# Seven-product groups between single blocks in five feed-forward networks, and 512-column weight splits in the mixers

## The chip, the cores and the metric

One core of one Trainium2 chip. The metric is device time of one execution in microseconds (us), lower is better. Engines: TensorE (PE, its weight loads PEld), VectorE (DVE), ScalarE (ACT), GpSimd (POOL); SyncE (SP) issues the loads.

## The reference

Two transformer blocks over 256 tokens of width 1024, in float32, with five feed-forward networks (FFNs) in all. Each FFN has 2816 hidden columns:

```python
    u = rms_norm(h, norm_ffn_g[l])
    g, up = jnp.split(u @ w_gate_up[l], 2, axis=-1)
    h = h + (jax.nn.silu(g) * up) @ w_down[l]
```

In order: a mixer (attention over 8 heads and an mLSTM, gated, with an output projection), an FFN with a norm behind it; then twice an FFN, a mixer (self attention and attention over 256 memory tokens, with an output projection) and an FFN. The four FFNs of the second part have the same form, with half the result added, `x + 0.5 * swiglu(...)`.

## The kernel before

Tokens stand in two tiles t of 128 rows. A product in float32 is made of three fp32r matmuls: every operand is split into a high part (a cast by ACT) and a low part (source minus high, by DVE), and `mm3` adds high x high, high x low and low x high into one PSUM bank of 512 columns. Activations are split once (`uh`, `ul`; `hh`, `hl` for the hidden block), weights while they stream.

Weights arrive in pieces of 128x2048 (1 MB), loaded in order on SP's queue into three `raw` tiles. Each piece is split in two halves of 1024 columns into `wh` and `wl`, six tiles of each (`W_BUFS`). `half(i, m, n)` hands a half to the matmuls, and makes sure that the splits of the next four jobs (`SPLIT_AHEAD`) have been issued. The order of the jobs is a list, filled beforehand by `plain` (a piece as it is) and `group_jobs`. PE's order is that of the program; ACT, DVE and the queues are ordered by the compiler by priority, with `crit()` moving work 300 places forward.

An FFN is cut into NJ = 11 blocks of 256 hidden columns. For a single block j, `gu(t, j)` runs 24 matmuls (gate and up, 512 columns, 8 row tiles of 128, three each) for each t; `element` makes the hidden block; `turn` transposes it (four 128x128 transposes, one set) and splits it; `dn(t, j)` adds its product with the down weights (12 matmuls for each t) into four PSUM banks that are kept for the whole FFN. So a single costs 72 matmuls. A set of transposes is put into PE's order by a hand-written clock (`side`), some us after the block that it belongs to.

A group takes two blocks j, j+1 with seven products instead of eight (2x2 blocks: token tile t by half of the 1024 inner rows; rows by hidden block). Its products P1, P6, P2, P5, P3, P7, P4 have 12 matmuls each and read sums of weights: DVE adds pieces for P6 (`t2`, four additions of 128x1024 in all), POOL's queue adds two more by accumulating transfers. Between the products stand the `dn` of two earlier blocks a, b, 24 matmuls each. A group costs 7 x 12 + 48 = 132 matmuls, and its results are joined by DVE. `group_operands`, after block 0, makes the sums of the activations.

Before the change an FFN runs five singles (0 to 4) and then three groups (5, 6), (7, 8), (9, 10), and then the down products of the last two blocks (48 matmuls, the tail), in which each of the last blocks is transposed and split in two parts, `turn((0,), j, ..)` and `turn((1,), j, ..)`, whose `hh` tiles have one buffer per t (`bufs=n`; two for the joint turn of both t). `fin(t)` adds the FFN's result to h, and `boundary` transposes and splits it for the next stage (eight transposes per t). `during` lets other work start inside the FFN: the parameters of the second part in the first FFN, the memory tokens' preparation (16 transposes and their splits) in the second and fourth.

The mixers split their 62 pieces (30, 16, 16) by the same code.

Of the kernel before, what the change touches and what calls it, by code (L numbers as in the profile page):

```python
# [19 lines left out]
NJ = 11  # L20
P_FFN = 3 * NJ
# [5 lines left out]
SPLIT_AHEAD = 4  # L27
LOAD_AHEAD = 2
CRIT = 300
SPLIT_W = 1024  # L30

GROUPS = 3

# [81 lines left out]
def kernel(  # L117
# [16 lines left out]
    pe, act, dve, pool = nc.tensor, nc.scalar, nc.vector, nc.gpsimd  # L134
    ctx.enter_context(tc.manual_schedule(engines={mybir.EngineType.PE}))
    side = Order()
# [57 lines left out]
    jobs, at_job = [], {}  # L194

    piece_at = {}

    def add_job(key, piece, work):

# [3 lines left out]
    def plain(i):  # L203
        for m in range(2):
            add_job((i, m), i, lambda i=i, m=m: raws[i][:, 1024 * m:1024 * m + 1024])
# [15 lines left out]
    def split(hi, lo, src):  # L221
        c = act.copy(out=hi, in_=src)  # L222
        dve.tensor_tensor(out=lo, in0=src, in1=hi.bitcast(F32), op=ALU.subtract)  # L223
        return c
# [3 lines left out]
    def in_order(inst):  # L228

        if order[0] is not None:  # L230
            tc.add_manual_dep(inst.ins, order[0].ins.name,
                              mybir.DependencyInfo(mybir.DependencyClass.NoSync, mybir.DependencyReason.DATA),
                              reason="order of the operands")
        order[0] = inst

    def split_to(n):

        while stream["split"] < min(n, len(jobs)):
            key, piece, work = jobs[stream["split"]]
            load_to(piece + 1 + LOAD_AHEAD)  # L240
            r = work()
            hi = wp.tile([128, 1024], FR, tag="wh", bufs=W_BUFS, name="wh")
            lo = wp.tile([128, 1024], FR, tag="wl", bufs=W_BUFS, name="wl")
            for s in range(0, 1024, SPLIT_W):
                in_order(split(hi[:, s:s + SPLIT_W], lo[:, s:s + SPLIT_W], r[:, s:s + SPLIT_W]))
            parts[key] = (hi, lo)
            stream["split"] += 1

# [5 lines left out]
    def group_jobs(i, pool_, dn):  # L254


        b11, b12, b22, b21 = i, i + 2, i + 3, i + 4
        kept[b12] = kept[b22] = pool_
        s = lambda m: slice(1024 * m, 1024 * m + 1024)
        total = []  # L260

        def job(name, piece, work):
            for m in range(2):
                add_job(((i, name), m), piece, lambda m=m: work(m))

        def add(out, a, b):
            dve.tensor_tensor(out=out, in0=a, in1=b, op=ALU.add)  # L267

        def t2(m):
            if m == 0:  # L270
                total.append(pool_[0].tile([128, 2048], F32, tag="tn", bufs=1, name="tn"))
            add(raws[b11][:, s(m)], raws[b11][:, s(m)], raws[b12][:, s(m)])
            add(total[0][:, s(m)], raws[b11][:, s(m)], raws[b22][:, s(m)])
            return total[0][:, s(m)]

        def dma_add(out, a):
            pool.dma_start(out=out, in_=a, accum_op=ALU.add)

        def b21_(m):
            if m == 0:  # L280
                dma_add(raws[b12], raws[b22])
            return raws[b21][:, s(m)]

        def b11_(m):
            if m == 0:
                dma_add(total[0], raws[b21])
            return raws[b11][:, s(m)]

        def t3(m):
            return raws[b12][:, s(m)]  # L290

        def t4(m):
            return total[0][:, s(m)]

        job("P1", b11, lambda m: raws[b11][:, s(m)])
        plain(dn[0])
        job("P6", b22, t2)
        job("P2", b21, b21_)
        job("P5", b21, b11_)
        plain(dn[1])  # L300
        job("P3", b21, lambda m: raws[b22][:, s(m)])
        job("P7", b21, t3)
        job("P4", b21, t4)
# [114 lines left out]
    def ffn_plan(p0):  # L418

        plan = {"pool": [None]}  # L420
        i = p0

        def source(key):
            kind, j = key
            if kind == "dn":
                return p0 + (3 * j + 4 if j < NJ - 1 else 32)
            return p0 if j == 0 else p0 + 3 * j - 1
        nc_ = NJ - 2 * GROUPS

        def take(key, n=1):  # L430
            nonlocal i
            plan[key] = i
            for q in range(n):
                piece_at[i + q] = source(key) + q
            i += n

        for j in range(nc_):
            take(("gu", j), 2)
            if 1 <= j < nc_ - 1:
                take(("dn", j - 1))  # L440
        for j in range(nc_):
            for q in range(2):
                plain(plan["gu", j] + q)
            if 1 <= j < nc_ - 1:
                plain(plan["dn", j - 1])
        for g in range(GROUPS):
            j = nc_ + 2 * g
            a, b = (j - 2, j - 1) if g == 0 else (j - 1, j - 2)
            plan["group", g] = i
            plan["dn", a], plan["dn", b] = i + 1, i + 5  # L450
            g0, g1 = source(("gu", j)), source(("gu", j + 1))
            piece_at.update(enumerate((g0, source(("dn", a)), g1, g1 + 1, g0 + 1, source(("dn", b))), i))
            group_jobs(i, plan["pool"], (i + 1, i + 5))
            i += 6
        for j in ((NJ - 2, NJ - 1) if GROUPS else ()):
            take(("dn", j))
            plain(plan["dn", j])
        assert i == p0 + P_FFN
        return plan

    def ffn_body(fp, p0, u, r, res_scale, finish, during=None):
        plan = plans[p0]
        plan["pool"][0] = fp
        accd = [None, None]
        hidT, hid_ready, hids = {}, {}, {}
        n_conv = NJ - 2 * GROUPS

        def element(t, j, acc):

# [8 lines left out]
        def gu(t, j):  # L478
            i = plan["gu", j]
            acc = lin(u[t], (i, i + 1))  # L480
            element(t, j, acc)
            if t == 1:
                side.spawn(turn((0, 1), j, 3.46))
            side.run()

# [63 lines left out]
            for name, t, k in (("P1", 0, 0), ("P2", 0, 4), ("P4", 1, 4)):  # L549
                S[name] = u[t][0][:, k:k + 4], u[t][1][:, k:k + 4]  # L550

        def group(g):

            j = n_conv + 2 * g
            a, b = (j - 2, j - 1) if g == 0 else (j - 1, j - 2)
            last = g == GROUPS - 1
            i = plan["group", g]

            def joined(x, y, op, into=None):
                o = fp.tile([128, 512], F32, tag="jo", bufs=4, name="jo") if into is None else into  # L560
                with crit():
                    dve.tensor_tensor(out=o, in0=x, in1=y, op=op)  # L562
                return o

            def prod(name):
                acc = bank()
                xh, xl = S[name]
                for k in range(4):
                    wh, wl = half((i, name), k // 2, 512)
                    mm3(acc, xh[:, k], xl[:, k], wh[:, k % 2], wl[:, k % 2], k == 0, k == 3)  # L570
                return acc

            c11 = fp.tile([128, 512], F32, tag="jo", bufs=4, name="jo")
            p1_ = prod("P1")
            with crit():
                act.copy(out=c11, in_=p1_)
            dn(1, a)
            dn(0, a)
            U = joined(prod("P6"), c11, ALU.add)
            joined(prod("P2"), c11, ALU.add, c11)  # L580
            element(0, j, c11)
            if last:
                side.spawn(turn((0,), j, 4.2))
            V = joined(prod("P5"), U, ALU.subtract)
            dn(0, b)
            c12 = joined(prod("P3"), V, ALU.add)
            element(0, j + 1, c12)
            if last:
                side.spawn(turn((0,), j + 1, 4.2))
            dn(1, b)  # L590
            p7 = prod("P7")
            joined(V, p7, ALU.subtract, V)
            element(1, j + 1, V)
            joined(p7, U, ALU.add, U)
            side.spawn(turn((1,) if last else (0, 1), j + 1, 4.9))
            joined(prod("P4"), U, ALU.add, U)
            element(1, j, U)
            side.spawn(turn((1,) if last else (0, 1), j, 4.2))

        for j in range(n_conv):  # L600
            more = 1 <= j < n_conv - 1
            gu(0, j)
            gu(1, j)
            if more:
                dn(0, j - 1)
                dn(1, j - 1)
            if j == 0:
                group_operands()
            if during and j == n_conv - 1:
                during()  # L610
        for g in range(GROUPS):
            group(g)
        j = NJ - 2
        dn(0, j)
        dn(1, j + 1, (0,))
        dn(0, j + 1, by_c=True)
        fin(0)
        dn(1, j + 1, (1,))
        dn(1, j, by_c=True)
        fin(1)  # L620


# [840 lines left out]
    u, r = first_mix(p)  # L1463
# [35 lines left out]
    for layer in range(2):  # L1499
# [7 lines left out]
        with tc.tile_pool(name=f"mix2_{layer}", bufs=1, reuse_waits="tile") as mixp:  # L1507
            u, r = second_mix(mixp, layer, p, nxt["u"], nxt["r"])
# [120 lines left out]
```

## Time and profile before

| | us |
|---|---|
| median of three runs | 1420.66 |
| the three runs | 1420.47, 1420.66, 4846.25 |
| profiled execution | 1421.74 |
| its span, first to last instruction | 1420.0 |
| PE busy in the span | 1369.3 |
| DVE busy | 1102.1 |
| ACT busy | 833.9 |
| POOL busy | 82.9 |

Matmuls overlap in the pipeline and their ends are modelled, so a share of busy time on PE does not tell how near it is to its rate; the distance from one matmul's start to the next does. A wait in a list of waits is idle time of an engine before an instruction, put down to what released it last. Span positions are us from the first instruction.

### The profile page before, as it was taken

The page shows a single profiled execution, that of the slowest core. Times are in us where ns is not written, and L with a number is a line of the kernel's source. Part 1 is how long each engine was busy: PE and PEld are TensorE (multiplying, and loading weights), DVE is VectorE, ACT ScalarE, POOL GpSimd, SP SyncE. Part 2 cuts the span into 40 slices and gives each one's busy share as a digit, 9 for nine tenths or more (in the row PEclk, how much of TensorE's full clock was granted, in tenths as well). Part 3 has the DMA queues.
Part 4 walks back from the last instruction along what each step waited for, and adds up shares of the span by engine and source line. Part 5 has one row for each costly group of instructions (what it writes and reads, how often), then busy time and mean ns, then how long its engine had stood idle before and what let it go on. Part 6 is the DMA issues. An engine that isn't in the chain of part 4 may idle for free.

```text
span 1420.0 us, 17210 instructions
## 1 busy us (share of the span) xinstructions
PE 1369.3 (96%) x6418; PEld 1093.1 (77%) x6418; DVE 1102.1 (78%) x1505; ACT 833.9 (59%) x1208; POOL 82.9 (6%) x89
## 2 busy tenths in 40 slices
PE   8999999999999999999999999999999989999998
PEld 7777888887778877777788877788777757788776
DVE  8866577689985899967585899866998777766897
ACT  6555545466664566567664566554666568554664
POOL 0000000000000000021000000000000111000000
PEclk9999999999999999999999999999999999999999
DMA  8433575477666667553365768656686432566683
GB/s 295 149 132 135 178 252 195 161 237 237 207 222 207 204 193 241 208 200 124 107 237 185 239 178 270 239 207 178 212 248 213 174 107 75 222 208 178 207 252 115
DMA packets 41395, 277.99 MB, mean 196 GB/s; under 512 B 5216, under 2 KB 6240, under 8 KB 8544
## 3 DMA queue, kind: packets, MB, share of 16 engines
q1 hardware_dynamic: 35568, 243.09, 47.2%
q0 software_dynamic: 4320, 31.46, 11.0%
q10 hardware_dynamic: 1424, 2.34, 0.5%
q8 instruction: 50, 0.82, 0.2%
q14 instruction: 33, 0.27, 0.1%
HBM read 244.37 MB, written 1.05 MB: 173 GB/s over the span
## 4 chain that ended last, share of the span: by engine, by line
PE 73%; DVE 18%; ACT 4%; issue 3%; POOL 1%; DMA 1%; DVEq 0%; POOLq 0%; ACTq 0%
PE bank L152 70%; DVE wl L223 8%; PE trbank L157 4%; ACT wh L222 2%; DVE tn L267 2%; POOL fac L341 1%; DVE jo L562 1%; DVE raw L267 1%; DVE hl L223 1%; DVE nm L645 1%; DMA mem<-in_mem_dram 1%; DVE hid L475 1%; DVE ms L1147 0%; ACT hh L222 0%; ACT p L647 0%
## 5 line engine op out<-in xcount | busy, mean ns | idle before, releaser
L223 DVE TENSOR_TENSOR wl<-raw,wh 128x1024 fp32r<-128x1024 f32 x424 | 512.9, 1221 | 132.1 <-ACT wh L222 123.3
L222 ACT CAST wh<-raw 128x1024 fp32r<-128x1024 f32 x424 | 439.0, 1050 | 176.9 <-PE bank L152 159.8
L152 PE MATMUL bank<-wh,uh 128*128 128x512 f32 x948 | 380.7, 402 | 2.2 <-ACT uh L222 2.0
L152 PE MATMUL bank<-wh,ul 128*128 128x512 f32 x948 | 374.5, 395 | 0.2 <-DVE ul L223 0.2
L152 PE MATMUL bank<-wl,uh 128*128 128x512 f32 x948 | 373.2, 394 | 0.0
L152 PEld LDWEIGHTS bank<-wh,uh 128*128 128x128 f32 x948 | 179.6, 189 | 41.9 <-ACT uh L222 2.4
L152 PEld LDWEIGHTS bank<-wh,ul 128*128 128x128 f32 x948 | 179.3, 189 | 40.9 <-DVE ul L223 1.1
L152 PEld LDWEIGHTS bank<-wl,uh 128*128 128x128 f32 x948 | 179.8, 190 | 36.9
L152 PE MATMUL bank<-wh,hh 128*128 128x512 f32 x440 | 176.6, 401 | 6.0 <-ACT hh L222 5.6
L152 PE MATMUL bank<-wh,hl 128*128 128x512 f32 x440 | 173.9, 395 | 4.0 <-DVE hl L223 3.9
L152 PE MATMUL bank<-wl,hh 128*128 128x512 f32 x440 | 173.3, 394 | 3.3 <-DVE wl L223 3.3
L222 ACT CAST wh<-tn 128x1024 fp32r<-128x1024 f32 x60 | 63.1, 1052 | 81.2 <-DVE tn L267 42.5
L152 PEld LDWEIGHTS bank<-wh,hl 128*128 128x128 f32 x440 | 82.6, 188 | 27.9 <-DVE hl L223 10.9
L152 PEld LDWEIGHTS bank<-wh,hh 128*128 128x128 f32 x440 | 82.7, 188 | 26.1 <-ACT hh L222 10.5
L152 PE MATMUL bank<-wl,sh 128*128 128x512 f32 x240 | 95.3, 397 | 6.8 <-DVE wl L223 6.8
L152 PEld LDWEIGHTS bank<-wl,hh 128*128 128x128 f32 x440 | 82.7, 188 | 23.7 <-DVE wl L223 7.6
L152 PE MATMUL bank<-wh,sh 128*128 128x512 f32 x240 | 95.2, 397 | 0.0
L152 PE MATMUL bank<-wh,sl 128*128 128x512 f32 x240 | 94.1, 392 | 0.0
L223 DVE TENSOR_TENSOR wl<-tn,wh 128x1024 fp32r<-128x1024 f32 x60 | 72.9, 1222 | 18.2 <-ACT wh L222 17.4
L223 DVE TENSOR_TENSOR wl<-rawx,wh 128x1024 fp32r<-128x1024 f32 x60 | 70.6, 1218 | 0.8 <-ACT wh L222 0.8
L473 ACT ACTIVATE th<-bank,r 128x256 f32<-128x256 f32 x50 | 23.7, 474 | 77.0 <-PE bank L152 77.0
L562 DVE TENSOR_TENSOR jo<-bank,jo 128x512 f32<-128x512 f32 x90 | 61.7, 686 | 2.1 <-PE bank L152 2.0
(248 smaller groups left out, 1534.0 us busy)
## 6 DMA issues: line engine op xcount, KB each, us to landing
raw<-in_weights_dram SPq DMA_DIRECT2D x196, 1024.0 KB, 4.9
rawx<-in_weights_dram SPq DMA_DIRECT2D x30, 1024.0 KB, 8.2
rawx<-rawx POOLq DMA_DIRECT2D x15, 1024.0 KB, 7.0
tn<-raw POOLq DMA_DIRECT2D x15, 1024.0 KB, 7.7
mem<-in_mem_dram ACTq DMA_DIRECT2D x4, 512.0 KB, 4.4
Tb<-in_rel_dram SPq DMA_DIRECT2D x3, 512.0 KB, 5.9
h<-in_x_dram SPq DMA_DIRECT2D x4, 256.0 KB, 3.8
raw<-in_weights_dram SPq DMA_DIRECT2D x2, 512.0 KB, 5.9
```

Of the source, the lines that this page charges most:

```text
L152: pe.matmul(out=out, lhsT=lhsT, rhs=rhs, start=start, stop=stop)
L157: pe.transpose(out=out, in_=in_, identity=ident if identity is None else identity)
L222: c = act.copy(out=hi, in_=src)
L223: dve.tensor_tensor(out=lo, in0=src, in1=hi.bitcast(F32), op=ALU.subtract)
L267: dve.tensor_tensor(out=out, in0=a, in1=b, op=ALU.add)
L341: pool.tensor_tensor(out=dst, in0=src, in1=mhalf[:, 0:n], op=ALU.pow)
L473: act.activation(out=th, in_=acc[:, 0:256], func=AF.Silu, scale=r[t])
L475: dve.scalar_tensor_tensor(out=hd, in0=acc[:, 256:512], scalar=r[t], in1=th, op0=ALU.mult, op1=ALU.mult)
L562: dve.tensor_tensor(out=o, in0=x, in1=y, op=op)
L645: dve.tensor_reduce(out=nm, in_=s, axis=AX.X, op=ALU.max, negate=True)
```

## The change

`BLOCKS` replaces `GROUPS`: an FFN runs singles 0 and 1, the group (2, 3), single 4, the group (5, 6), single 7, the group (8, 9), and single 10. The down products are taken from a list `todo`: a group carries those of two earlier blocks, a single that of one, and the FFN ends with those of blocks 9, 8 and 10. The last single is transposed in two parts, one for each t; all other blocks for both t together. `during` runs after the fifth of the eight entries, the group (5, 6), instead of after single 4. Pieces of FFNs are noted in `of_ffn` and still split 1024 columns at a time; all others, those of the mixers, 512 at a time.

```diff
-SPLIT_W = 1024
-GROUPS = 3
+SPLIT_W, SPLIT_W_FFN = 512, 1024
+BLOCKS = ((0,), (1,), (2, 3), (4,), (5, 6), (7,), (8, 9), (10,))
...
-            for s in range(0, 1024, SPLIT_W):
-                in_order(split(hi[:, s:s + SPLIT_W], lo[:, s:s + SPLIT_W], r[:, s:s + SPLIT_W]))
+            w = SPLIT_W_FFN if piece in of_ffn else SPLIT_W
+            for s in range(0, 1024, w):
+                in_order(split(hi[:, s:s + w], lo[:, s:s + w], r[:, s:s + w]))
...
+        of_ffn.update(range(p0, p0 + P_FFN))
...
+        todo = []
+        for block in BLOCKS:
+            j = block[0]
+            down = plan["down", j] = [] if len(todo) < 2 else [todo.pop(0) for _ in block]
+            if len(block) == 1:
+                take(("gu", j), 2)
+                for x in down:
+                    take(("dn", x))
+                todo.append(j)
+            else:
+                a, b = down
+                plan["group", j], plan["dn", a], plan["dn", b] = i, i + 1, i + 5
...
+                group_jobs(i, plan["pool"], (i + 1, i + 5))
+                i += 6
+                todo += [j + 1, j]
+        plan["down", None] = todo
+        for x in todo:
+            take(("dn", x))
...
-            if t == 1:
+            if j == BLOCKS[-1][0]:
+                side.spawn(turn((t,), j, 3.46))
+            elif t == 1:
                 side.spawn(turn((0, 1), j, 3.46))
...
-            if last:
-                side.spawn(turn((0,), j, 4.2))
...
-            side.spawn(turn((1,) if last else (0, 1), j + 1, 4.9))
+            side.spawn(turn((0, 1), j + 1, 4.9))
...
-            side.spawn(turn((1,) if last else (0, 1), j, 4.2))
+            side.spawn(turn((0, 1), j, 4.2))
...
+        def single(j):
             gu(0, j)
             gu(1, j)
-            if more:
-                dn(0, j - 1)
-                dn(1, j - 1)
-            if j == 0:
+            for x in plan["down", j]:
+                dn(0, x)
+                dn(1, x)
+
+        for n, block in enumerate(BLOCKS[:-1]):
+            if len(block) == 1:
+                single(block[0])
+            else:
+                group(block[0])
+            if n == 0:
                 group_operands()
-            if during and j == n_conv - 1:
+            if during and n == len(BLOCKS) // 2:
                 during()
-        for g in range(GROUPS):
-            group(g)
-        j = NJ - 2
-        dn(0, j)
-        dn(1, j + 1, (0,))
-        dn(0, j + 1, by_c=True)
+        j = BLOCKS[-1][0]
+        x, = plan["down", j]
+        y, z = plan["down", None]
+        gu(0, j)
+        dn(0, x)
+        gu(1, j)
+        dn(1, x)
+        dn(0, y)
+        dn(1, y, (0,))
+        dn(0, z, by_c=True)
         fin(0)
-        dn(1, j + 1, (1,))
-        dn(1, j, by_c=True)
+        dn(1, y, (1,))
+        dn(1, z, by_c=True)
         fin(1)
```

## Rows read from the trace of the kernel before

**Rows 1.** Timeline of PE: start us, us, engine, line, operation, tiles
```profile
773.72 0.39 PE L152 MATMUL bank<-wl,uh 128*128 128x512 f32 x1
...
776.00 0.39 PE L152 MATMUL bank<-wh,ul 128*128 128x512 f32 x1
```

**Rows 2.** Busy time by stage of the third FFN, columns as headed
```profile
core 0: us, PE busy (x) PEld busy (x) DVE busy (x) ACT busy (x) POOL busy (x), PEclk, DMA share, GB/s
721.85:745.16 23.31, 23.31 (x110) 19.25 (x109) 20.62 (x28) 15.72 (x22) 1.47 (x1) 1.00 0.72 271
745.16:762.08 16.92, 16.92 (x78) 13.91 (x76) 8.84 (x10) 7.64 (x9) 0.00 (x0) 1.00 0.53 187
...
795.93:826.40 30.47, 30.47 (x137) 25.09 (x136) 25.58 (x28) 20.48 (x23) 0.86 (x1) 1.00 0.77 254
826.40:859.34 32.94, 31.94 (x142) 25.48 (x142) 31.79 (x36) 21.17 (x25) 1.72 (x2) 1.00 0.75 233
859.34:893.80 34.46, 32.85 (x146) 25.65 (x144) 32.80 (x37) 22.49 (x27) 1.72 (x2) 1.00 0.72 214
893.80:908.76 14.96, 13.06 (x61) 10.00 (x60) 11.69 (x17) 6.69 (x11) 0.56 (x1) 1.00 0.59 197
```

**Rows 3.** Waits of PE's weight loads, 826.40 to 908.76: us, times, longest
```profile
PEld bank L152 <- DVE wl L223: 3.4, 4, 1.1
PEld bank L152 <- DVE hl L223: 2.5, 4, 1.0
PEld bank L152 <- ACT hh L222: 2.2, 3, 1.3
```

**Rows 4.** Busy time of the five FFNs from the end of gu(1,1)
```profile
236.84:404.14 167.30, 161.25 (x710) 127.88 (x708) 135.15 (x150) 95.36 (x116) 5.98 (x7) 1.00 0.66 213
429.48:597.06 167.58, 162.03 (x725) 129.36 (x724) 137.85 (x155) 96.47 (x119) 6.35 (x8) 1.00 0.67 212
745.16:908.76 163.60, 159.09 (x709) 127.97 (x708) 132.79 (x146) 93.75 (x113) 5.79 (x7) 1.00 0.67 213
933.46:1100.16 166.70, 161.52 (x726) 129.47 (x724) 137.81 (x155) 96.28 (x119) 7.25 (x8) 1.00 0.66 213
1254.97:1416.20 161.23, 157.95 (x701) 127.03 (x699) 127.25 (x140) 87.72 (x105) 5.23 (x6) 1.00 0.62 193
```

**Rows 5.** Timeline of DVE at the end of the third FFN's first group
```profile
821.06 1.22 DVE L223 TENSOR_TENSOR wl<-raw,wh 128x1024 fp32r<-128x1024 f32 x1
...
822.59 2.36 DVE L223 TENSOR_TENSOR wl<-raw,wh 128x1024 fp32r<-128x1024 f32 x2
...
826.53 1.22 DVE L223 TENSOR_TENSOR wl<-raw,wh 128x1024 fp32r<-128x1024 f32 x1
```

**Rows 6.** Waits of PE between the first and the second FFN
```profile
PE bank L152 <- ACT uh L222: 2.0, 1, 2.0
```

**Rows 7.** Timeline of DVE early in the fourth FFN
```profile
930.62 2.60 DVE L223 TENSOR_TENSOR wl<-raw,wh 128x1024 fp32r<-128x1024 f32 x2
...
935.10 1.23 DVE L223 TENSOR_TENSOR wl<-raw,wh 128x1024 fp32r<-128x1024 f32 x1
```

**Rows 8.** Groups by shape, 512 columns: count, busy us, mean ns, idle
```profile
L223 DVE TENSOR_TENSOR sl<-uf,sh 128x512 fp32r<-128x512 f32 x20 | 12.8, 684 | 0.0
...
L222 ACT CAST sh<-uf 128x512 fp32r<-128x512 f32 x20 | 11.6, 618 | 1.1 <-DVE uf L544 0.9 <-DVE uf L545 0.3
```

**Rows 9.** Page, costliest groups: the two halves of a 1024-column split
```profile
L223 DVE TENSOR_TENSOR wl<-raw,wh 128x1024 fp32r<-128x1024 f32 x424 | 512.9, 1221 | 132.1 <-ACT wh L222 123.3
L222 ACT CAST wh<-raw 128x1024 fp32r<-128x1024 f32 x424 | 439.0, 1050 | 176.9 <-PE bank L152 159.8
```

**Rows 10.** Timeline of DVE, four 512-column subtractions in a row
```profile
420.54 2.49 DVE L223 TENSOR_TENSOR sl<-uf,sh 128x512 fp32r<-128x512 f32 x4
```

**Rows 11.** Busy time in the three mixers
```profile
12.40:213.30 200.90, 197.93 (x981) 158.30 (x981) 140.32 (x269) 108.49 (x170) 3.04 (x7) 1.00 0.53 184
609.00:721.85 112.85, 107.60 (x598) 84.20 (x596) 74.32 (x140) 72.95 (x157) 14.28 (x13) 0.97 0.41 145
1112.11:1231.66 119.55, 110.14 (x579) 84.99 (x578) 84.40 (x158) 74.61 (x162) 16.82 (x14) 0.97 0.38 133
```

More of the change, by code (lines that the diff above doesn't have):

```diff
@@ L196 @@
     piece_at = {}
+    of_ffn = set()
     def add_job(key, piece, work):
@@ L427, in source @@
             return p0 if j == 0 else p0 + 3 * j - 1
-        nc_ = NJ - 2 * GROUPS
+        of_ffn.update(range(p0, p0 + P_FFN))
         def take(key, n=1):
@@ L434, in take @@
                 piece_at[i + q] = source(key) + q
+                plain(i + q)
             i += n
[L437 to L445, printed above, removed]
-        for g in range(GROUPS):
[L447 to L457, printed above, removed]
+        todo = []
[10 more added lines that the diff above has]
+                plan["group", j], plan["dn", a], plan["dn", b] = i, i + 1, i + 5
+                g0, g1 = source(("gu", j)), source(("gu", j + 1))
+                piece_at.update(enumerate((g0, source(("dn", a)), g1, g1 + 1, g0 + 1, source(("dn", b))), i))
+                group_jobs(i, plan["pool"], (i + 1, i + 5))
[4 more added lines that the diff above has]
+            take(("dn", x))
         assert i == p0 + P_FFN
@@ L465, in ffn_body @@
         hidT, hid_ready, hids = {}, {}, {}
-        n_conv = NJ - 2 * GROUPS
         def element(t, j, acc):
@@ L550, in group_operands, with group @@
                 S[name] = u[t][0][:, k:k + 4], u[t][1][:, k:k + 4]
[L552 to L557, printed above, removed]
+        def group(j):
+            a, b = plan["down", j]
+            i = plan["group", j]
             def joined(x, y, op, into=None):
@@ L587, in group @@
             element(0, j + 1, c12)
-            if last:
-                side.spawn(turn((0,), j + 1, 4.2))
             dn(1, b)
@@ L594, in group @@
             joined(p7, U, ALU.add, U)
-            side.spawn(turn((1,) if last else (0, 1), j + 1, 4.9))
+            side.spawn(turn((0, 1), j + 1, 4.9))
             joined(prod("P4"), U, ALU.add, U)
             element(1, j, U)
-            side.spawn(turn((1,) if last else (0, 1), j, 4.2))
-        for j in range(n_conv):
-            more = 1 <= j < n_conv - 1
+            side.spawn(turn((0, 1), j, 4.2))
+        def single(j):
             gu(0, j)
             gu(1, j)
-            if more:
-                dn(0, j - 1)
-                dn(1, j - 1)
-            if j == 0:
+            for x in plan["down", j]:
[7 more added lines that the diff above has]
+            if n == 0:
                 group_operands()
-            if during and j == n_conv - 1:
+            if during and n == len(BLOCKS) // 2:
                 during()
-        for g in range(GROUPS):
-            group(g)
-        j = NJ - 2
-        dn(0, j)
-        dn(1, j + 1, (0,))
-        dn(0, j + 1, by_c=True)
+        j = BLOCKS[-1][0]
+        x, = plan["down", j]
+        y, z = plan["down", None]
+        assert z == j
+        gu(0, j)
[5 more added lines that the diff above has]
+        dn(0, z, by_c=True)
         fin(0)
-        dn(1, j + 1, (1,))
-        dn(1, j, by_c=True)
+        dn(1, y, (1,))
+        dn(1, z, by_c=True)
         fin(1)
```

## The prediction

> **What bounds the kernel now.** I read the profile's page first: TensorE (PE) shows as busy nearly throughout, VectorE (DVE) comes next. Since a busy PE is not PE at its peak, I went to the distance between matmul starts in the timeline. In an undisturbed stretch the 128x512 matmuls start 0.228 us apart (ten steps from 773.72 to 776.00) [rows 1], so PE's floor can be counted. A single block (72 matmuls and one set of four transposes of 128x128) took 16.92 us [rows 2]; 72 x 0.228 = 16.42, so a set of four costs about 0.48.
>
> The table by stage shows where an FFN leaves that floor. In the third FFN the single block and the first seven-product group run at it (16.92 us; 30.47 for 132 matmuls and one set, 30.1 + 0.48 = 30.6). The second group, with two sets (31.06), took 32.94, the third, with a little more, 34.46, and the tail of 48 matmuls 14.96, where 10.9 and four sets' worth of transposes are 12.9 [rows 2]. So the loss is not in the groups as such. It grows from group to group, and the tail adds its own.
>
> The list of waits says who is late in those three stretches (826.40 to 908.76): PE's weight load waits 3.4 us for wl (the low parts of the split weights, made by DVE), and 2.5 and 2.2 us for hl and hh (the transposed hidden block) [rows 3]. In a single DVE is busy 8.84 of 16.92 us, in groups two and three 31.79 of 32.94 and 32.80 of 34.46 [rows 2]. So three groups in a row spend DVE's lead, while singles in a row leave DVE idle, since it may be only a few splits ahead.
>
> **The floor of an FFN.** From the end of gu(1,1) the FFN has 756 - 96 = 660 matmuls, ten turns of four transposes, and eight transposes at its end: 660 x 0.228 + 12 x 0.48 = 156.3 us. The second and fourth FFN carry 16 transposes of the memory tokens (4 x 0.48 = 1.9, so 158.2); the last one lacks the eight (155.3). Measured from there: 167.30, 167.58, 163.60, 166.70, 161.23 [rows 4]. The excess is 11.0 + 9.4 + 7.3 + 8.5 + 5.9 = 42.1 us. That is the pool the reordering can draw on. The matmul count is unchanged: five singles and three groups, as before.
>
> **The change, part by part.**
>
> *Group after a single.* The splits of a group's first product and first down block, and the additions for P6, can be made while the single runs. The first group of the third FFN already stands behind a single and loses nothing. All such groups should run like it: the wl waits go. DVE's mean load allows it (132.79 of 163.60 us [rows 4]; over the 156.3 it would be 85%).
>
> *Single after a group.* New: gu(0,j) wants four half pieces within four times 6 matmuls (1.37 us each), where a following group wanted two and then two at 2.7. The first group of the third FFN shows the lead: the next four wl were started at 821.06, 822.59 (two of them) and 826.53 and were done by about 822.3, 823.8, 825.0 and 827.8 [rows 5]. In the new order they would be needed from the stretch's end at 826.40 [rows 2], 1.37 apart: at 826.4, 827.8, 829.1 and 830.5. They have over 2.7 us in hand. Cost taken: 0; without that cover up to the 1.1 us of another split each.
>
> *hh and hl.* Before, the first down product of groups two and three comes straight after P1, on a block whose transposes stood at P1's end; now a single's gu pair of 11 us lies between. These waits go.
>
> *The tail.* Before, the last two blocks are transposed in four parts with one buffer per token half, so a part's split waits for the previous down product; that is most of the tail's 2 us [rows 2]. Now the last block is a single, one part per buffer, and its down product comes after those of blocks 9 and 8. Gone.
>
> *What stays or comes.* (a) After the first FFN, PE waits 2.0 us for the next block's uh [rows 6], which hangs on a chain of row sums and scales that starts when h is ready, not on PE; PE arrives about 1 us earlier (the longest of the hh waits, 1.3 [rows 3], stood in the tail), so it waits about 3.0; with the matmul behind it I keep 3.4 of that FFN's excess. (b) The first group now follows gu 0 and 1. In the third FFN DVE had 2.7 us idle there (20.62 of 23.31 [rows 2]). Where FFN follows FFN it is tighter: in the fourth, the splits that become P1's and the down block's ran from 930.62 on, the last of the four from 935.10, with P1 due at 933.46 [rows 7]. From about 936.2 DVE then has four additions and two splits of 1.14 (the step in [rows 5]) and an hl of 0.6 (512 columns, [rows 10]) for P6, 7.4 in all, done at 943.6; P6's second half is due at 933.46 + 8.2 (36 matmuls) + 0.5 (a set) + 1.4 (6 matmuls) = 943.5. I charge 1.0 in each of the two. (c) The memory tokens' preparation is spawned two blocks later, by its waits half of it beside single 7 and half beside the last group: 0.5 each. (d) 0.5 per FFN for steps of 0.1 that stand at starts of runs. Kept: 3.4 + 2 x 1.5 + 5 x 0.5 = 8.9 us.
>
> *A new wait.* hh of singles 4 and 7 takes the buffer that the preceding dn(1,x) still reads, so ScalarE's (ACT's) copy, placed early as urgent, stands up to 2 us, and behind it the copies for P6. P6 is due 8 us later: 0.
>
> *Moved.* Each FFN's pieces, loads on SP's queue, the two accumulating transfers per group on POOL's, and SPLIT_AHEAD are the same in number. The second block's parameters wait only for small loads and can fill idle DVE time anywhere. Cost 0.
>
> *Mixers.* 62 pieces, 124 halves, are split by two instructions of 512 on ACT and DVE instead of one of 1024. No 512-column split of weights is in the trace; the nearest rows are sl<-uf (684 ns) and sh<-uf (618 ns) against 1221 and 1050 [rows 8, 9]. By durations a half costs DVE 147 and ACT 186 ns more, 18.2 and 23.1 us in all. By starts it is less: four sl in a row took 2.49 us, a step of 0.603 [rows 10], against 1.14 for the wide one [rows 5]: 0.066 per half, 8.2 us. DVE is busy 299 of 433 us in these stretches, ACT 256 [rows 11], and a half is used for 2.7 us of matmuls: hidden, unless it delays the attention's short instructions. These in turn wait behind a narrower split. PE's idle time there is 3.0 + 5.3 + 9.4 = 17.6 us [rows 11]; halved at best, -8.8. I take 0 with ends -9 and +18, since DVE and ACT have slack but short chains cut both ways.
>
> [...]
>
> **Sum.** 42.1 - 8.9 = 33.2 us off the FFNs, 0 in the mixers. The profiled execution took 1421.74 us with a span of 1420.0, the median of the runs is 1420.66, so the sum can be set against the median: 1420.66 - 33.2 = 1387.5, say 1387.
>
> **Rivals.**
> - *The mixers pay for the narrow splits.* +8 to +18 on the path: 1395 to 1405. For: DVE is busy 140 of 201 us in the first mixer, and its order is fixed. Against: the slack in [rows 11]. Chance 0.15. [...]
> - *The lead is not rebuilt, so the reordering does not do its work.* The wl waits (3.4 per FFN, 17 us) stay: 1404. For: the lead is bounded by six buffers. Against: the first group behind a single. Chance 0.10.
> - *Slower than before.* The group's last joins, hidden halves and splits leave none of the four halves ready when gu starts. Place: each of 15 changes from group to single. If all four splits come after it, DVE needs 4 x 1.14 plus about 3 us of joins, hid and hl, and ACT's 1.05 before them: 8.6 against PE's 5.5, so 3.1 us and more; 15 x 3.1 = 47, 1434. It cancels the gain from 33.2 / 15 = 2.2 us on. [Rows 5] stands against it. Chance 0.05.
> - *Narrow splits unblock the attention chains.* -9: 1378. Chance 0.10.
>
> **Numbers.** Forecast 0.60, within 1381 to 1393. Two per cent (about what a measurement of this kernel can tell from no change) is 28.4 us, a time below 1392.3. Faster: 0.60 x 0.95 + 0.10 = 0.67; slower, the far end of the third rival, 0.03; within 2% the rest, 0.30. The range takes in the fourth rival and the first up to the second's 1404: 1376 to 1404.
>
> **What would show it.** Groups near 30 to 31.5 us in every FFN, and wl nearly gone from the list of PE's waits; tails without hh and hl waits; FFNs from gu 1's end at about 156 to 160 us; the uh wait after the first FFN near 3 us; mixers within a few us of [rows 11]. Wrong: wl waits at the first product of each single after a group, ACT standing at hh, P6 late in the first group by more than 2 us, or mixers longer by 8 us.

## The result and the profile after

The changed kernel took 1374.11 us (median), the kernel before 1420.57 beside it: ratio 0.968, 95% interval 0.966 to 0.970, 46.5 us less. The forecast was 1387, with a range from 1376 to 1404. So the direction came as forecast, and the runs below bear out the cause, but the time lies 2 us below the range: the gain was 46.5 us where 33.2 had been worked out.

The chain that ended last shows the change in one line. It runs through TensorE for 90% of the span, and VectorE's part has gone from 18% to 6%. First the line of the kernel before:

```profile
PE 73%; DVE 18%; ACT 4%; issue 3%; POOL 1%; DMA 1%; DVEq 0%; POOLq 0%; ACTq 0%
```

and that of the changed kernel:

```profile
PE 90%; DVE 6%; POOL 1%; ACT 1%; issue 1%; DMA 0%; DVEq 0%; POOLq 0%; ACTq 0%
```

The table by stage of the changed kernel answers to [rows 2, 4, 11]. The first seven lines are the third FFN: the gu products of blocks 0 and 1, the first group, single 4, group, single 7, group, and single 10 with the tail. Then come the five FFNs from the end of gu(1,1), and the three mixers.

```profile
core 0: us, PE busy (x) PEld busy (x) DVE busy (x) ACT busy (x) POOL busy (x), PEclk, DMA share, GB/s
697.13:720.44 23.31, 23.31 (x110) 19.25 (x108) 23.00 (x30) 15.73 (x22) 1.47 (x1) 1.00 0.62 226
720.44:750.94 30.50, 30.50 (x137) 25.12 (x136) 27.31 (x30) 21.05 (x24) 1.78 (x2) 1.00 0.87 277
750.94:768.78 17.84, 17.84 (x86) 14.71 (x85) 15.10 (x18) 9.10 (x12) 0.00 (x0) 1.00 0.57 195
768.78:798.78 30.00, 30.00 (x133) 24.71 (x132) 26.23 (x28) 20.56 (x23) 1.72 (x2) 1.00 0.89 281
798.78:816.63 17.85, 17.85 (x85) 14.72 (x85) 15.11 (x18) 9.11 (x12) 0.00 (x0) 1.00 0.51 176
816.63:846.63 30.00, 30.00 (x133) 24.71 (x132) 26.23 (x28) 20.55 (x23) 1.72 (x2) 1.00 0.72 211
846.63:876.29 29.66, 29.66 (x141) 24.52 (x141) 19.75 (x26) 15.63 (x22) 0.56 (x1) 1.00 0.63 227
...
234.30:392.55 158.25, 158.25 (x710) 128.66 (x708) 129.96 (x142) 95.70 (x112) 5.96 (x7) 1.00 0.71 231
416.65:575.01 158.36, 158.03 (x725) 130.06 (x724) 137.49 (x159) 99.32 (x123) 10.06 (x9) 1.00 0.70 229
720.44:876.29 155.85, 155.85 (x709) 128.49 (x708) 129.72 (x143) 96.00 (x113) 5.78 (x7) 1.00 0.72 235
899.69:1057.38 157.69, 157.69 (x725) 130.10 (x724) 135.03 (x156) 99.89 (x123) 8.62 (x7) 1.00 0.71 230
1213.14:1368.07 154.93, 154.93 (x701) 127.47 (x699) 124.68 (x137) 89.17 (x104) 5.21 (x6) 1.00 0.65 207
...
12.30:210.98 198.68, 198.11 (x981) 158.57 (x981) 144.18 (x330) 113.67 (x227) 2.66 (x5) 1.00 0.52 186
586.96:697.13 110.17, 105.35 (x597) 83.39 (x596) 75.30 (x164) 74.56 (x180) 15.92 (x13) 0.98 0.42 149
1069.33:1189.84 120.51, 109.86 (x580) 85.78 (x579) 86.24 (x183) 77.07 (x185) 18.79 (x14) 0.96 0.36 123
```

Two things are to be seen. In the third FFN PE is busy in every stretch from end to end, where the second and third group and the tail had gaps of 1.0, 1.6 and 1.9 us [rows 2]; all three groups are nearly alike, 30.0 to 30.5 us. And DVE's load is even: 26.23 of 30.00 us in a group, 15.1 of 17.85 in a single. Before it was 31.8 and 32.8 in the late groups and 8.8 in a single [rows 2]. The work is spread and hardly reduced: over the whole third FFN DVE was busy 153.4 us before and 152.7 after.

The list of what PE's weight loads wait for, over all that follows the first mixer, has one wait for wl left, and none for hh or hl (one FFN alone had the eleven of [rows 3]):

```profile
PEld trbank L158 <- issue: 8.4, 7, 3.9
...
PEld bank L153 <- DVE wl L225: 0.8, 1, 0.8
```

Where the time went, by stages cut at the first matmul of each, in us (the same cut for all kernels; the experiments follow below):

| stage | before | after | order only | width only | groups in a row |
|---|---|---|---|---|---|
| first mixer | 201.13 | 198.68 | 201.11 | 199.34 | 198.69 |
| FFN 1, from gu(1,1)'s end | 167.30 | 158.25 | 158.25 | 167.29 | 162.62 |
| FFN 2, gu of blocks 0 and 1 | 25.35 | 24.10 | 24.10 | 23.70 | 24.12 |
| FFN 2, rest | 167.58 | 158.36 | 158.42 | 166.77 | 164.33 |
| second mixer | 112.83 | 110.17 | 110.12 | 108.09 | 109.77 |
| FFN 3, rest | 163.60 | 155.85 | 155.90 | 163.58 | 160.85 |
| FFN 4, gu of blocks 0 and 1 | 24.70 | 23.40 | 23.41 | 25.46 | 23.40 |
| FFN 4, rest | 166.70 | 157.69 | 157.69 | 165.73 | 164.25 |
| third mixer | 119.55 | 120.51 | 119.47 | 120.00 | 121.38 |
| FFN 5, rest | 161.25 | 154.92 | 154.97 | 161.24 | 159.99 |
| span | 1419.95 | 1372.58 | 1373.59 | 1409.94 | 1399.85 |

The span is 47.4 us shorter: 41.3 in the five rests (826.4 to 785.1), 2.55 in the gu products at the two places where FFN follows FFN, 4.15 net in the mixers (-2.45, -2.66, +0.96), 0.1 at the start, and 0.8 lost behind the last FFN.

### The profile page after: what moved, and what is told of

Read it like the earlier page. It is cut to its first block, busy times and chain, and to the rows that moved or that the text cites. A ratio compares the mean times of both kernels' runs of the same rounds, so it can differ in the third digit from the quotient of the medians.

```text
span 1372.6 us, 17475 instructions
## 1 busy us (share of the span) xinstructions
PE 1347.2 (98%) x6418; PEld 1094.7 (80%) x6418; DVE 1106.1 (81%) x1624; ACT 853.4 (62%) x1327; POOL 90.4 (7%) x89
## 3 DMA queue, kind: packets, MB, share of 16 engines
HBM read 244.37 MB, written 1.05 MB: 179 GB/s over the span
## 4 chain that ended last, share of the span: by engine, by line
PE 90%; DVE 6%; POOL 1%; ACT 1%; issue 1%; DMA 0%; DVEq 0%; POOLq 0%; ACTq 0%
PE bank L153 85%; PE trbank L158 5%; DVE wl L225 2%; POOL fac L344 1%; DVE nm L654 1%; DVE ms L1156 0%; DVE z L1160 0%; DVE p L666 0%; ACT wh L224 0%; DVE p L652 0%; ACT p L656 0%; DMA cst<-in_consts_dram 0%; DVE z L1218 0%; DVE z L1220 0%; DVE h L1490 0%
## 5 line engine op out<-in xcount | busy, mean ns | idle before, releaser
L225 DVE TENSOR_TENSOR wl<-raw,wh 128x1024 fp32r<-128x1024 f32 (+1 forms) x548 | 522.0, 978 | 82.9 <-ACT wh L224 76.5
L224 ACT CAST wh<-raw 128x1024 fp32r<-128x1024 f32 (+1 forms) x548 | 454.9, 856 | 126.2 <-PE bank L153 118.4
L224 ACT CAST hh<-trbank 128x512 fp32r<-128x512 f32 (+1 forms) x60 | 33.0, 551 | 62.8 <-PE trbank L158 58.9
L224 ACT CAST wh<-rawx 128x1024 fp32r<-128x1024 f32 x60 | 63.0, 1054 | 13.3 <-PE bank L153 10.8
```

## The experiments

**The order alone.** The changed kernel, with the mixers' splits at their old width:

```diff
-SPLIT_W, SPLIT_W_FFN = 512, 1024
+SPLIT_W, SPLIT_W_FFN = 1024, 1024
```

> The new block order alone; the mixers split 1024 columns as before. By the stage tables of before and after, the mixers took about 4 us less after the change (first mixer 2.5, second 2.7, third -1.0), the FFNs with the stages between them about 42. Theory (width makes the mixers' difference): about 1378 us, with the first mixer's end back near its old place. Rival (the mixers moved because of their new surroundings, not the width): 1374. Rival (the width is worth more than the mixers show, through the boundaries): above 1382.

Measured: 1376.98 us, ratio 0.969 (0.968 to 0.970). The FFNs are those of the changed kernel to 0.1 us (table). So the order makes nearly all of the gain. What is left for the width, 2.9 us, is not clear of the two intervals (0.968 to 0.970 here, 0.966 to 0.970 for both changes). By stages the first mixer went back to 201.1 us and the third to 119.5, as the theory had it; the second did not go back to 112.8.

**The width alone.** The kernel before, with 512-column splits in the mixers:

```diff
-SPLIT_W = 1024
+SPLIT_W, SPLIT_W_FFN = 512, 1024
...
+            w = SPLIT_W_FFN if piece in of_ffn else SPLIT_W
+            for s in range(0, 1024, w):
...
+        of_ffn.update(range(p0, p0 + P_FFN))
```

> The old block order with 512-column splits in the mixers. Theory (width is worth 4 us, all in the mixers): 1416 to 1417 us. Rival (added fixed cost per instruction on the path, as I allowed for in the prediction): 1428 to 1438. Rival (no effect): 1420.

Measured: 1412.88 us, ratio 0.994 (0.993 to 0.995), 8.0 us less, twice the theory's gain. Its trace gives 1.8 us in the first mixer and 4.7 in the second, where PE's granted clock was 1.00 in this execution against 0.97 [rows 11]; 1.65 in the gu products ahead of FFN 2's rest, which differ by as much between two executions of the kernel before (last section); 0.8 and 1.0 in FFNs 2 and 4; 1.2 lie ahead of the first mixer, and FFN 4's gu products and the third mixer were 0.8 and 0.45 longer. None of the three forecasts on record held. Order alone (43.9) and width alone (8.0) add up to 52, both together gave 46.5. What the width does on the old order beyond the first mixer stays open.

**A quarter of the width**, 256 columns in the mixers, on the new order:

```diff
-SPLIT_W, SPLIT_W_FFN = 512, 1024
+SPLIT_W, SPLIT_W_FFN = 256, 1024
```

> The changed kernel with 256-column splits in the mixers, 1024 in the FFNs. If a narrower split helps because urgent short instructions wait behind it for less long, the mixers' waits shrink a little more: 1371 to 1374 us. If the fixed cost per instruction counts, four narrow ones cost DVE about 0.14 us more per half than two, 17 us over the mixers, and ACT more: 1376 to 1390.

Measured: 1379.06 us, ratio 0.971 (0.969 to 0.972), 5 us above the changed kernel. So narrower is not better without end. Most of the 5 us stands in the second mixer, 114.15 us at a granted clock of 0.97 against 110.17 at 0.98; the first is 1.45 longer. The stage table of this kernel's first mixer:

```profile
13.02:213.15 200.13, 198.21 (x982) 158.60 (x981) 151.93 (x450) 123.50 (x343) 2.58 (x3) 1.00 0.53 184
```

and that of the order alone, with 1024 columns, together with the waits of PE in it (us, times, longest):

```profile
12.52:213.62 201.10, 198.14 (x981) 158.51 (x981) 140.53 (x270) 108.87 (x169) 3.03 (x7) 1.00 0.53 183
```

```profile
PE trbank L158 <- DVE ms L868: 1.7, 1, 1.7
PE trbank L158 <- DVE at L781: 1.3, 1, 1.3
```

In the changed kernel one wait of PE stands in the first mixer:

```profile
PE trbank L158 <- DVE rd L864: 0.6, 1, 0.6
```

With wide splits two transposes wait 3.0 us for short DVE instructions, with 512 columns one waits 0.6: 2.4 less, which is the stage's gain (201.10 to 198.68). The same lines tell what a narrow split costs DVE: 60 instructions more made it busy 144.18 instead of 140.53, 120 more 151.93 instead of 144.18, so 61 and 65 ns for each. With 256 columns there is one wait of 1.6 us for DVE's rs in this stage.

Each half has two instructions more with 256 columns than with 512, so it costs DVE 0.13 us more, where the expectation had 0.14. The durations of single instructions would make it more than twice that: 686 ns with 512 columns and 417 with 256, against 1219 for the few of 1024 columns in this stretch, which is 148 to 153 ns for each further instruction where the engine's busy time says 61 to 65. Back to back the end of one overlaps the start of the next: the 512-column subtractions last 684 ns and start 603 ns apart [rows 8, 10]. For DVE's load the busy time decides.

**512 columns everywhere**, in the FFNs too:

```diff
-SPLIT_W, SPLIT_W_FFN = 512, 1024
+SPLIT_W, SPLIT_W_FFN = 512, 512
```

> The changed kernel with 512-column splits in the FFNs too. By starts a half costs DVE 0.066 us more, 84 halves per FFN: 5.5 us on top of some 133 in 156, still under the span. Theory (DVE's mean load decides, and there is room): 1374 to 1378 us, no wl waits in groups. Rival (the groups' margin is thinner than the mean says, or ACT's 0.14 to 0.19 per half counts in groups, where it is paced at one half per 1.37 us): wl waits return, 1382 to 1400.

Measured: 1376.61 us, ratio 0.969 (0.967 to 0.971). FFN 1 is 1.2 us longer and the gu products behind it 0.8, the other FFNs change by at most 0.7, and no wl wait comes back. The even order has DVE time to spare for it (with 1024 columns DVE is busy 129.72 of 155.85 us in FFN 3).

**512 columns in one mixer, and in two.** In the first mixer alone:

```diff
-            w = SPLIT_W_FFN if piece in of_ffn else SPLIT_W
+            w = SPLIT_W if piece < 30 else SPLIT_W_FFN
```

> The changed kernel with 512-column splits in the first mixer only (pieces 0 to 29), 1024 elsewhere. In the runs so far the first mixer takes 198.7 to 199.3 us with 512 columns and 201.1 with 1024 in every kernel, the last mixer 118.9 to 121.4 with 512 and 119.5 to 120.6 with 1024. Theory (the width's gain is in the first and second mixer, the third gains nothing or loses up to 1 us): first mixer about 198.9, second 110 at full granted clock and 112.8 below it, third 119.5 to 120.5; total within 2 us of the changed kernel. Rival (the widths of the mixers interact through the compiler's order): first mixer off 199 by over 1 us.

Measured: 1374.82 us, ratio 0.968 (0.967 to 0.969). First mixer 198.68, third 119.50: each stage goes with its own width. In the first and second:

```diff
-            w = SPLIT_W_FFN if piece in of_ffn else SPLIT_W
+            w = SPLIT_W if piece < 112 and piece not in of_ffn else SPLIT_W_FFN
```

> The changed kernel with 512-column splits in the first and second mixer and 1024 in the third and in the FFNs, the best width of each stage by the stage tables so far. If the stages add up as they stand: first mixer 198.7 us, second 108 to 110.2 by its granted clock, third 119.5, and 0.7 to 1.6 us less than the changed kernel in all, about 1373. Rival (the third mixer's small differences come from elsewhere): the time of the changed kernel, third mixer 120 to 121.4.

Measured: 1374.51 us, ratio 0.967 (0.966 to 0.969): not to be told from the changed kernel. So the gain that the stage tables promised, 0.7 to 1.6 us, was not seen. The third mixer took 119.53 us, as with 1024 columns elsewhere, but the second mixer came out at 111.35 here, at a granted clock of 0.97. No tried kernel beats the changed one by more than its interval.

**New tail, groups in a row.** The changed kernel with its last single, but the three groups side by side:

```diff
-BLOCKS = ((0,), (1,), (2, 3), (4,), (5, 6), (7,), (8, 9), (10,))
+BLOCKS = ((0,), (1,), (2,), (3,), (4, 5), (6, 7), (8, 9), (10,))
```

> The changed kernel with its blocks in the old sequence, singles 0 to 3, groups (4,5), (6,7), (8,9) in a row, and only the last single moved behind them. It has the new tail without the alternation. Theory (alternation takes away the wl, hh and hl waits of groups two and three, about 5 us per FFN): 1374 + 25 = about 1399 us, with wl waits in the third group and none in the tail. Rival (the tail is the larger part): 1380 to 1388.

Measured: 1398.59 us, ratio 0.984 (0.982 to 0.986). The rests of the FFNs add up to 812.0 us, against 826.4 before and 785.1 after. So in the profiled executions the new end of the FFN is worth 14.4 us, and the alternation behind it 27.0. The profiled execution of this kernel was the slowest of its four (1401.66 us); by the medians the alternation is worth 24.5 (1398.59 less 1374.11). The second group in a row and the stretch from single 10 on, in this kernel's third FFN:

```profile
core 0: us, PE busy (x) PEld busy (x) DVE busy (x) ACT busy (x) POOL busy (x), PEclk, DMA share, GB/s
...
798.05:831.00 32.95, 31.99 (x142) 25.50 (x141) 31.80 (x37) 21.18 (x25) 1.72 (x2) 1.00 0.78 252
...
859.44:891.84 32.40, 32.40 (x153) 26.74 (x152) 22.90 (x30) 17.83 (x24) 0.56 (x1) 1.00 0.61 227
```

and the waits of its weight loads over that FFN:

```profile
PEld bank L153 <- DVE wl L225: 3.4, 4, 1.1
PEld bank L153 <- DVE hl L225: 1.3, 2, 0.9
PEld bank L153 <- ACT hh L224: 0.9, 2, 0.5
```

The second group takes 32.95 us with DVE busy 31.80: [rows 2] again, and the wl waits are the 3.4 us of [rows 3] to the digit. The end has no gap (32.40 of 32.40). The two parts of the prediction's mechanism show separately: the waits inside the groups stay, those of the tail go. The alternation with the old end was not run, so the two shares hold in this order only.

**A fourth group in the row**, with 12 matmuls fewer in each FFN:

```diff
-BLOCKS = ((0,), (1,), (2, 3), (4,), (5, 6), (7,), (8, 9), (10,))
+BLOCKS = ((0,), (1,), (2, 3), (4, 5), (6, 7), (8, 9), (10,))
```

> Four groups in a row behind singles 0 and 1, single 10 last: 12 matmuls fewer per FFN, 5 x 12 x 0.228 = 13.7 us less on PE. If the lead sufficed: about 1361 us. Theory (DVE falls behind in each group that follows a group, by some 2 to 3.5 us as in the old order's second and third): 1361 + 5 x 3 x 2.5 = about 1398. This shows what a single between groups is worth against a saved product.

Measured: 1399.67 us, ratio 0.986 (0.983 to 0.988). 60 matmuls fewer than the kernel with three in a row (5 x 12, 60 x 0.228 = 13.7 us) gained nothing: the fourth group brought three more wl waits and one more each for hl and hh (2.5, 0.4 and 0.5 us more than with three in a row), as its weight loads show:

```profile
PEld bank L153 <- DVE wl L225: 5.9, 7, 1.1
PEld bank L153 <- DVE hl L225: 1.7, 3, 0.9
PEld bank L153 <- ACT hh L224: 1.4, 3, 0.5
```

The third FFN took 161.0 us where its PE was busy 156.9. In this kernel a fourth group saves PE's work but not time, as DVE isn't given the time to prepare it. Four groups with singles between them were not tried.

**The boundary alone.** The prediction let the wait for uh behind the first FFN grow. In the kernel before, DVE has the scaling of h for later use ahead of the product that uh is made from (start, us, engine, line, operation, tiles):

```profile
400.29 1.22 DVE L1481 TENSOR_TENSOR h<-h,gf 128x1024 f32<-128x1024 f32 x1
401.42 0.68 DVE L382 TENSOR_TENSOR uf<-trbank,gfin 128x512 f32<-128x512 f32 x1
```

In the changed kernel the two stand the other way round, and PE waits for nothing there:

```profile
390.22 0.69 DVE L385 TENSOR_TENSOR uf<-trbank,gfin 128x512 f32<-128x512 f32 x1 [0.45 <-PE trbank L158]
390.83 1.22 DVE L1490 TENSOR_TENSOR h<-h,gf 128x1024 f32<-128x1024 f32 x1
```

So I gave the kernel before that order, by having the code that issues the scaling, `after()` in `boundary`, come later:

```diff
+                yield 2.0
                 after()
```

> The kernel before, with the first FFN's closing scale work (the row sums, the product of h with the norm's gain and the rescaling) issued 2 us later on the hand-written clock; nothing else is changed. In the prediction I held that the 2.0 us wait for uh after the first FFN hangs on that chain, whatever PE does. Theory now (the product of h, 1.2 us on DVE, merely stood ahead of uf in DVE's fixed order): the wait falls to under 0.7 us, and the time by 2 to 3 us, with the half-rate matmuls behind it. Rival (the chain itself sets it): the wait stays near 2.0 or grows, the time is unchanged.

Measured: 1418.56 us, ratio 0.998 (0.997 to 0.999). The uh wait is gone, uf runs at 400.62 without h<-h,gf in front of it, and FFN 1 ends 2.2 us earlier (167.30 to 165.11):

```profile
400.62 0.68 DVE L382 TENSOR_TENSOR uf<-trbank,gfin 128x512 f32<-128x512 f32 x1
```

Part of it comes back later. The chain that was put off also makes the scale r that th reads in FFN 2, and there PE waits once for 1.7 us for jo, where the kernel before waits 0.2 us, and 0.8 when run again; FFN 2's rest took 168.93 us against 167.58 and 168.14.

The kernel with the groups in a row has no wait of PE at this place either, so it goes with the new end of the FFN, not with the alternation.

**Both kernels once more**, unchanged, to see how far a stage differs between executions:

> The changed kernel itself, profiled once more. Theory: whether PE's granted clock falls after the second mixer's waits differs from execution to execution, and with it 2 to 2.7 us; then the second mixer comes out at 108.1 us with a granted clock of 1.00 or again at 110.2 with 0.98, the first mixer and the FFNs within 0.1 us of the first profile. Rival (the dip belongs to the kernel): 110.2 and 0.98 again, and other kernels' 108.1 are theirs.

> The kernel before, profiled once more. By the same theory the second mixer comes out at 112.8 us with 0.97 or near 110 with 1.00 (as the order-only kernel and the late-residual kernel, which split 1024 columns there too); the first mixer at 201.1 and the FFNs at 167.3, 167.6, 163.6, 166.7, 161.2 as in the first profile, each within 0.5 us but for the first matmuls behind the wait after the first FFN.

Measured: 1376.69 and 1420.1 us, one run each. The first mixer and the FFNs come back within 0.2 us for the changed kernel (0.6 for the one before), but the second mixer does not: 112.14 us at a granted clock of 0.97, where the same kernel had 110.17 at 0.98; and for the kernel before 111.33 at 0.98 against 112.85 at 0.97 [rows 11]. Neither the values named by the theory nor those of its rival came. The lines of the two repeats, changed kernel first:

```profile
586.75:698.89 112.14, 106.64 (x598) 84.41 (x596) 75.28 (x164) 74.57 (x180) 15.44 (x13) 0.97 0.43 146
```

```profile
608.54:719.87 111.33, 106.04 (x598) 83.25 (x596) 74.23 (x140) 72.87 (x157) 14.26 (x13) 0.98 0.42 147
```

Differences of up to 2 us in the second mixer are therefore nothing that one profile can settle. At equal clock 512 columns are some 0.7 to 2 us shorter there: 108.1 (width alone) against 110.1 (order alone) at 1.00, 110.2 (after) against 111.3 (before) and 111.8 (512 in the first alone) at 0.98, 111.35 (512 in two) and 112.14 (after) against 112.85 (before) at 0.97. One wait of PE goes with the width in every profile: with 1024 columns it waits 0.9 to 1.0 us for rs in the second mixer, with 512 never. Here it is in the kernel before:

```profile
PE trbank L157 <- DVE rs L650: 1.0, 1, 1.0
```

Not tried: a second buffer for the transposed parts in the old tail, which would have shown what the buffer alone does there.

## Where the prediction was right, and where its sum failed

**Floor and pool: right in the sum.** The rests stand at the counted floor: 158.25, 158.36, 155.85, 157.69 and 154.93 against 156.3, 158.2, 156.3, 158.2 and 155.3. Together that is 785.1 against 784.3, so 41.3 of the pool of 42.1 us came. That the two agree so closely is partly luck: FFN 1 stands 1.95 above its floor, for a reason that the floor doesn't have (last section), and FFNs 3 to 5 together 1.3 below theirs. By the prediction's own figures a set of transposes costs 0.50 and not 0.48 (16.92 less 16.42), which makes the pool 1.3 us smaller.

**Group after a single, hh and hl: right.** Groups near 30 to 31.5 us were named, and wl nearly, hh and hl wholly gone from the waits; the third FFN's took 30.0 to 30.5, and of the waits one for wl is left, in FFN 2. **The tail: right**, and worth more than the 2 us each that were seen: by the groups in a row 4.7, 3.25, 2.75, 2.45 and 1.3 us in the five FFNs, 14.4 in all. About 2 us of FFN 1's share is the uh wait; what the rest above 10 is made of isn't shown.

**Single after a group, cost 0: right.** The halves for single 4 in the third FFN are due from 750.94 on, 1.37 us apart. DVE, at the end of the first group:

```profile
745.60 1.22 DVE L225 TENSOR_TENSOR wl<-raw,wh 128x1024 fp32r<-128x1024 f32 x1
...
747.14 2.35 DVE L225 TENSOR_TENSOR wl<-raw,wh 128x1024 fp32r<-128x1024 f32 x2
...
750.61 1.22 DVE L225 TENSOR_TENSOR wl<-raw,wh 128x1024 fp32r<-128x1024 f32 x1
```

They are done by 746.8, 748.3, 749.5 and 751.8, against 750.9, 752.3, 753.7 and 755.1: over 3 us in hand, where [rows 5] gave 2.7. The rival in which this change of block becomes the new bound is refuted, and so is the one in which the lead isn't rebuilt.

**The new wait at hh, cost 0: right.** The foreseen wait, for matmuls that still read the buffer, is there twice in each FFN, but short: 0.2 us in the third FFN, 1.05 at most, where up to 2 were named. Longer are ACT's waits for the transposes themselves (20.3 us in 14 waits before). Both over the whole run of the changed kernel, from what ACT sat idle for before hh:

```profile
PE trbank L158: 58.9, 45
...
PE bank L153: 4.0, 10
```

Nothing stands behind them that PE waits for: its one wl wait is in FFN 2's first group, before single 4.

**"Kept: 8.9 us": the step that failed.** Measured 0.8 (785.1 less 784.3), and by its parts:

- *(a) 3.4 for the uh wait.* I held that its chain starts when h is ready and would stay, so that an earlier PE waits longer. But 1.2 of its 2.0 us were one DVE instruction, h<-h,gf, which the compiler's order had put in front. In the new order it stands behind, and there is no wait. The old kernel with that one edit shows it, in a wait that fell from 2.0 us to 0.2. A wait that hangs on an engine's fixed order is not anchored to its data; the line above the late instruction in DVE's timeline would have shown it.
- *(b) 1.0 for the first group of FFNs 2 and 4.* I let all four additions for P6 run after P1's splits. In the fourth FFN two of them are done before P1 starts at 899.69, and P6's two splits end at 903.8 and 905.5, over 4 us before they are due (P1's start + 8.2 + 0.5 = 908.4, and 1.4 later):

```profile
895.37 2.35 DVE L270 TENSOR_TENSOR raw<-raw,rawx 128x1024 f32<-128x1024 f32 x2
...
902.57 1.22 DVE L225 TENSOR_TENSOR wl<-tn,wh 128x1024 fp32r<-128x1024 f32 x1
...
904.22 1.23 DVE L225 TENSOR_TENSOR wl<-tn,wh 128x1024 fp32r<-128x1024 f32 x1 [0.42 <-ACT wh L224]
```

  I had taken DVE's order from a schedule in which singles followed, and put the additions behind it. In FFN 2 they do stand there: all four run after P1's start at 416.65, and P6's second split ends at 426.47, 0.2 us before it is due at 426.71. PE's one wl wait follows in that group, at its second down block, and costs 0.3 us. So the order was right for one of the two FFNs, and its price too high.
- *(c), (d) 0.5 here and there, 3.5 in all.* Hardly any of it is to be seen: FFN 2 stands 0.2 us above its floor, FFNs 3 to 5 0.4 to 0.5 below. FFN 1 alone is 1.95 above, for a reason of its own (last section).

**Where FFN follows FFN: not in the sum.** The rests end with the first matmul of what follows, and I took the gu products of the next one as unchanged. In FFN 4 they went from 24.70 to 23.40 us, 0.87 of it idle time of PE that is gone. FFN 2's 1.25 us are within what one kernel showed in two executions (25.35 and 23.70).

**Mixers, 0 with ends -9 and +18: mis-sized by a few us.** DVE's load rose by the forecast's small step (61 to 65 ns an instruction against the 66 taken from starts) and was hidden. But the short instructions of the attention did come through earlier, the fourth rival's mechanism: 2.4 us in the first mixer, shown by its waits. The second gained 0.7 to 2 at equal clock, 1.0 of it the wait for rs. The third lost 1.0: its listed waits add up to 10.5 us in the changed kernel and 9.4 with 1024 columns. One wait goes, one comes and one grows. With 512 columns (changed kernel):

```profile
PE trbank L158 <- DVE p L1255: 3.8, 1, 3.8
...
PE trbank L158 <- ACT wh L224: 1.7, 1, 1.7
```

With 1024 (order alone):

```profile
PE trbank L158 <- DVE rs L659: 3.2, 1, 3.2
PE trbank L158 <- DVE p L1255: 1.5, 1, 1.5
```

**The sum.** Forecast and span differ by 14.2 us: 8.1 of the kept term, 4.15 of the mixers, 2.55 of the gu products, less 0.7 at the two ends of the run. The kept term is the sure part. The mixers' gain is 4.15 us in this profile and 1.5 in the second profile of the same kernel (432.0 us against 433.5 before), and of the gu products' 2.55 only FFN 4's 1.3 is clear of the spread. The first alone would have given 1379, inside the range; the range missed because it was widened for late splits and costly mixers, and hardly for the possibility that nothing is kept and the mixers gain as well.

## What to carry to other kernels

Where two kinds of blocks load a helper engine unequally and its lead is bounded, mix them: the same work cost some 25 us less with the heavy blocks one by one between light ones, and a saving in matmuls (four groups in a row) was worth nothing without it. That the buffers bound the lead is read from waits (ACT's splits wait 183.6 us for PE in the changed kernel); no run changed their number. Count the bound engine's floor from its undisturbed step and ask of each wait that you mean to keep which instruction stands before it on its engine: if that one isn't needed there, the wait may go with any reordering, though part of it may turn up later. Narrow instructions on a helper engine were a trade of its short chains against its load (first mixer: 2.4 us less from 1024 to 512 columns, 1.45 more from 512 to 256); try one step, stage by stage.

## What the hardware showed that was not expected

PE's rate behind a short wait was not the same in two executions of one kernel. In the kernel before, PE waited 2.0 us for uh ahead of FFN 2 in both. In the first, the 3.86 us behind it had a granted clock of 0.71, and the slowest matmuls in it started 0.42 to 0.43 us apart, 1.9 times the 0.228 of [rows 1]:

```profile
404.14:408.00 3.86, 3.86 (x13) 2.79 (x14) 2.69 (x6) 3.50 (x5) 2.01 (x2) 0.71 1.03 435
```

In the second the granted clock was 1.00, and 20 instructions fitted where 13 had:

```profile
404.75:408.61 3.86, 3.86 (x20) 2.99 (x21) 3.42 (x8) 3.54 (x6) 2.01 (x2) 1.00 1.04 437
```

The gu products of blocks 0 and 1 took 25.35 and 23.70 us. The second mixer's spread of 2 us went with its granted clock too: 110.17 us at 0.98 and 112.14 at 0.97 in the changed kernel.

FFN 1 runs slower than the other four at a granted clock of 1.00: in the changed kernel its matmuls start 0.232 us apart on the mean (distances under 0.3 us, transposes left out), 0.228 in the others, and the kernel before shows the same (0.232 in FFN 1, 0.228 to 0.229 in the others). Over 660 matmuls that is some 2.4 us; it stands 1.95 above its floor where FFNs 3 to 5 stand 0.4 to 0.5 below. The cause wasn't found.
